# RMSNorm with repeated rows: squares in wide instructions, whole-tile copies on ScalarE, gamma on the loads' queue

## The chip, the cores and the metric

The kernel runs on one core of one Trainium2 chip. The time is that of one execution on the device, in microseconds (us). The kernel before takes 239.57 us (median of 3 runs, 239.40 to 239.84). A profile covers one execution; its span is some 2 us shorter than the time of the same run (237.9 and 239.72 us for the kernel before). A transfer is issued to a queue, moves as packets, and lands: in these traces a whole load is 128 packets of 32 KiB, a store 128 packets of 64 KiB, and each has 16 landing records. The profile counts 16 DMA engines, and this text reads the 16 records as one for each.

## The reference

```python
def reference(x, gamma):                      # x: 8 x 512 x 2048, gamma: 2048, fp32
    x_rep = np.repeat(x, 2, axis=1)           # each row twice
    rms = np.sqrt((x_rep ** 2).mean(axis=-1, keepdims=True) + 1e-6)
    return (x_rep / rms * gamma[None, None, :]).astype(np.float32)
```

It reads 33.6 MB and writes 67.1 MB. There are 4096 rows to normalise; each is written twice.

## The kernel before

Eight tiles of 128 partitions and 4 rows each. A tile's buffer has 8 rows per partition: `x` is loaded into the upper 4, the results go to rows 0, 2, 4, 6 and are then copied to rows 1, 3, 5, 7. There are three buffers, so load 3 waits for store 0 (load 3 is issued at 52.84 us, store 0's last landing record is at 52.82), load 4 for store 1, and so on.

```python
    def square(i, k):                # ScalarE: sum of squares of one row, then the root
        sq = junk.tile([P, D], f32, name="sq")            # in PSUM
        nc.scalar.activation(out=sq[:], in_=ys[i][:, K * (R - 1) + k, :],
                             func=Act.Square, accum_out=ss[:])
        nc.scalar.activation(out=rms[:], in_=ss[:], func=Act.Sqrt, scale=inv_d, bias=eps_t[:])
        # ... cut: allocation of ss, rms and rstd; square returns rms
    def scale(i, k, rms):            # VectorE: x * (1/rms) * gamma
        nc.vector.reciprocal(out=rstd[:], in_=rms[:])
        nc.vector.scalar_tensor_tensor(out=ys[i][:, R * k, :], in0=ys[i][:, K * (R - 1) + k, :],
                                       scalar=rstd[:], in1=gamma_b[:], op0=Alu.mult, op1=Alu.mult)
    def compute(i):
        for k in range(K):
            scale(i, k, square(i, k))
        repeat(i, 0, K // 2, nc.scalar.copy)
        repeat(i, K // 2, K, nc.vector.tensor_copy)
    # ... cut
    load(0, nc.sync, parts=2)
    for c0, c1 in zip(cuts, cuts[1:]):                    # 7 pieces of gamma, ScalarE's queue
        nc.scalar.dma_start(out=gamma_b[0:1, c0:c1], in_=gamma[c0:c1].partition_broadcast(1))
    nc.gpsimd.partition_broadcast(out_ap=gamma_b[:], in_ap=gamma_b[0:1, :])
    # ... cut: eps_t
    load(1, nc.sync); load(2, nc.sync)                    # (two lines in the source)
    loads_after = {2: (3, 4, 5), 4: (6, 7)}
    for i in range(ntiles):
        compute(i)
        store(i, 0, K)
        for j in loads_after.get(i, ()):
            load(j, nc.sync)
```

So the one queue of the sync engine carries, in this order: loads 0, 1, 2, stores 0, 1, 2, loads 3, 4, 5, stores 3, 4, loads 6, 7, stores 5, 6, 7.

## Time and profile before

| | before |
|---|---|
| time, median | 239.57 us |
| span of the profiled run | 237.9 us |
| VectorE (DVE) busy | 96.5 us, 41% |
| ScalarE (ACT) busy | 101.0 us, 42% |
| loads' and stores' queue, share of 16 DMA engines | 98.5% |
| rate over the span | 423 GB/s |

The prediction below shows the page, the stretches and the chain. The timeline of the sync engine's queue: start, length, line, what was issued and how many times.

```profile
27.05 24.67 SPq L56 DMA_DIRECT2D out_dram<-y  x3
52.84 39.05 SPq L52 DMA_DIRECT2D y<-in_x_dram  x3
115.86 12.72 SPq L56 DMA_DIRECT2D out_dram<-y  x2
140.24 19.73 SPq L52 DMA_DIRECT2D y<-in_x_dram  x2
```

Store 3 is issued at 115.86 and store 4 some 12.4 us later; their first packets move at 119.4 and 138.7 us, so both are there in time. The table by stretches (columns: length, busy time of VectorE, ScalarE and GpSimd with the number of instructions, clock, DMA share, GB/s) at 176 to 178 us, where load 7 ends and store 5 begins:

```profile
176.00:178.00 2.00, 1.96 (x3) 2.00 (x3) 0.00 (x0) 1.00 1.43 606
```

A packet is booked whole in the stretch in which it begins. The 606 GB/s are therefore no rate; they say that many of the 64 KiB packets of store 5 (10 by the packet records) began within these 2 us, beside the last 17 of load 7.

### The profile page before, as it was taken

How to read it: one execution, taken by the hardware profiler on the slowest of the kernel's cores; microseconds unless marked ns; L12 is line 12 of the kernel's file. 1: busy time of each engine (PE TensorE's matmuls, PEld its weight loads, DVE VectorE, ACT ScalarE, POOL GpSimd, SP SyncE). 2: the span in 40 equal slices, each digit the busy share in tenths (PEclk: the TensorE clock that was granted, in tenths of full speed). 3: DMA queues.
4: the chain of work that ended last, by engine and by line, in shares of the span. 5: the costliest groups of instructions: out<-in, count | busy, mean ns of one | idle time of the engine just before them, and what ended most of it. 6: DMA issues, size and time to landing. Idle time of an engine off the chain costs nothing.

```text
span 237.9 us, 287 instructions
## 1 busy us (share of the span) xinstructions
DVE 96.5 (41%) x73; ACT 101.0 (42%) x106; POOL 2.5 (1%) x5
## 2 busy tenths in 40 slices
DVE  0049999960000000059999960000199990000000
ACT  2697999900000000099999920000599960000000
POOL 0030000000000000000000000000000000000000
DMA  7999998989899998999998999989998989999994
GB/s 265 436 446 441 441 441 353 530 353 496 386 452 430 397 485 353 441 441 441 441 518 364 464 419 430 452 369 430 435 518 364 518 364 485 397 452 430 408 474 176
DMA packets 2464, 100.69 MB, mean 423 GB/s; under 512 B 279, under 2 KB 285, under 8 KB 286
## 3 DMA queue, kind: packets, MB, share of 16 engines
q1 hardware_dynamic: 2448, 100.66, 98.5%
q14 instruction: 2, 0.02, 0.0%
q10 hardware_dynamic: 14, 0.01, 0.0%
HBM read 33.56 MB, written 67.11 MB: 423 GB/s over the span
## 4 chain that ended last, share of the span: by engine, by line
DMA 58%; ACT 12%; DVE 9%; issue 1%; POOLq 1%; ACTq 1%; SPq 0%
DMA y<-in_x_dram 33%; DMA out_dram<-y 21%; ACT sq L64 8%; DVE y L74 7%; DMA gamma_b<-in_gamma_dram 4%; ACT y L81 3%; DVE y L81 2%; ACT rms L68 1%; POOLq L136 1%; ACTq L95 1%; DVE rstd L73 0%; POOLq L96 0%; SPq L56 0%
## 5 line engine op out<-in xcount | busy, mean ns | idle before, releaser
L64 ACT ACTIVATE sq<-y 128x2048 f32<-128x2048 f32 x32 | 59.7, 1865 | 87.8 <-DMA y<-in_x_dram 87.8
L74 DVE SCALAR_TENSOR_TENSOR y<-y,rstd,gamma_b 128x2048 f32<-128x2048 f32 x32 | 75.3, 2352 | 4.1 <-POOL gamma_b L96 3.0
L73 DVE RECIPROCAL rstd<-rms 128x1 f32<-128x1 f32 x32 | 5.0, 158 | 94.6 <-ACT rms L68 94.3
L81 ACT COPY y<-y 128x4096 f32<-128x4096 f32 x8 | 28.7, 3590 | 1.4 <-DVE y L74 1.4
L81 DVE COPY y<-y 128x4096 f32<-128x4096 f32 x8 | 18.3, 2294 | 0.3
L68 ACT ACTIVATE rms<-ss,eps_t 128x1 f32<-128x1 f32 x32 | 9.4, 295 | 1.0
L64 ACT ACTIVATION_READ_ACCUMULATOR sq<-y 128x1 f32 x32 | 6.0, 187 | 0.0
L64 ACT ACT_TABLE_LOAD x1 | 1.3, 1283 | 3.0 <-issue 3.0
L96 POOL PARTITION_BROADCAST gamma_b<-gamma_b x1 | 2.3, 2294 | 12.2 <-DMA y<-in_x_dram 12.2
L68 ACT ACT_TABLE_LOAD x1 | 1.3, 1283 | 0.0
L98 DVE MEMSET eps_t<- 128x1 f32 x1 | 0.1, 59 | 0.8 <-PEq L125 0.8
L125 POOL MEMSET const-uint8-127<- 128x1 uint8 x1 | 0.1, 102 | 0.0
L125 POOL MEMSET const-bfloat16-1.0<- 128x1 bf16 x1 | 0.1, 101 | 0.0
L125 POOL MEMSET const-float32-0.0<- 128x1 f32 x1 | 0.1, 98 | 0.2 <-issue 0.2
L125 POOL MEMSET const-float32-1.0<- 128x1 f32 x1 | 0.1, 98 | 0.0
## 6 DMA issues: line engine op xcount, KB each, us to landing
y<-in_x_dram SPq DMA_DIRECT2D x7, 4096.0 KB, 14.6
y<-in_x_dram SPq DMA_DIRECT2D x2, 2048.0 KB, 7.4
out_dram<-y SPq DMA_DIRECT2D x8, 24.4
gamma_b<-in_gamma_dram ACTq DMA_DIRECT2D x6, 1.0 KB
gamma_b<-in_gamma_dram ACTq DMA_DIRECT2D x1, 2.0 KB
```

The source lines that it names most:

```text
L64: nc.scalar.activation(out=sq[:], in_=ys[i][:, K * (R - 1) + k, :], func=Act.Square, accum_out=ss[:])
L68: nc.scalar.activation(out=rms[:], in_=ss[:], func=Act.Sqrt, scale=inv_d, bias=eps_t[:])
L73: nc.vector.reciprocal(out=rstd[:], in_=rms[:])
L74: nc.vector.scalar_tensor_tensor(out=ys[i][:, R * k, :], in0=ys[i][:, K * (R - 1) + k, :], scalar=rstd[:], in1=gamma_b[:], op0=Alu.mult, o ...
L81: copy(out=y_r[:, k0:k1, 1, :], in_=y_r[:, k0:k1, 0, :])
L95: nc.scalar.dma_start(out=gamma_b[0:1, c0:c1], in_=gamma[c0:c1].partition_broadcast(1))
L96: nc.gpsimd.partition_broadcast(out_ap=gamma_b[:], in_ap=gamma_b[0:1, :])
L98: nc.vector.memset(eps_t, eps)
L125: nc = _bacc.Bacc("TRN2", target_bir_lowering=False, num_devices=1)
L136: with _tile.TileContext(nc) as tc:
```

## The change

Its intent is fewer and longer instructions. Tiles 2, 5, 7 ("wide") are squared by one instruction of 8192 elements into the free lower half of their own buffer, and VectorE sums them. Tiles 1, 4, 6 ("half") do this for two rows and keep the accumulating square (one instruction that squares a row and sums it) for the other two. Tiles 0 and 3 ("rows") keep four accumulating squares, with one root for two rows. ScalarE takes over nearly all copies. Gamma's pieces go on the loads' queue: six between the halves of tile 0's load, the seventh behind them.

```diff
-    def square(i, k):
+    def total(i, k, ss):                       # accumulating square of one row, to PSUM
+    def square(i, k0, k1):                     # rows k0..k1 in one instruction, to SBUF
+        nc.scalar.activation(out=ys[i][:, k0:k1, :],
+                             in_=ys[i][:, x_at + k0 : x_at + k1, :], func=Act.Square)
+    def reduce(i, k0, k1, ss):
+        nc.vector.tensor_reduce(out=ss[:, k0:k1], in_=ys[i][:, k0:k1, :], op=Alu.add, ...)
+    def rows_tile(i, copy=nc.vector.tensor_copy):
+        for k0 in (0, H):
+            for k in range(k0, k0 + H):
+                total(i, k, ss)
+            rsqrt(k0, k0 + H, ss, rstd)
+            scale(i, k0, k0 + H, rstd)
+        repeat(i, 0, H)
+        repeat(i, H, K, copy)
 ... (cut: half_tile, wide_tile, rsqrt)
-    load(0, nc.sync, parts=2)
+    load_half(y0, 0)
+    for c0, c1 in zip(cuts[:-2], cuts[1:-1]):
+        gamma_piece(c0, c1)                    # on nc.sync
+    load_half(y0, 1)
+    gamma_piece(cuts[-2], cuts[-1])
-    for i in range(ntiles):
-        compute(i)
-        store(i, 0, K)
+    rows_tile(0);  store(0, 0, K)
+    half_tile(1);  square(2, 0, K);  repeat(1, 0, K);  store(1, 0, K)
+    wide_tile(2);  repeat(2, 0, K);  store(2, 0, K)
+    load(3), load(4), load(5)
+    rows_tile(3);  store(3, 0, K)
+    half_tile(4);  square(5, 0, K);  repeat(4, 0, H);  repeat(4, H, K);  store(4, 0, K)
+    load(6), load(7)
+    wide_tile(5);  repeat(5, 0, K);  store(5, 0, K)
 ... (cut: tiles 6 and 7 likewise; several statements are put on one line here)
```

More of the change, by code (lines that the diff above doesn't have):

```diff
@@ L43, with load_half, load @@
     ys = []
-    def load(i, eng, parts=1):
+    def load_half(y, h):
+        k0 = h * (K // 2)
+        at = K * (R - 1) + k0
+        nc.sync.dma_start(out=y[:, at : at + K // 2, :], in_=x_t[0, :, k0 : k0 + K // 2, :])
+    def load(i):
         y = rows.tile([P, K * R, D], f32, name="y")
-        step = K // parts
-        for k in range(0, K, step):
-            at = K * (R - 1) + k
-            eng.dma_start(out=y[:, at : at + step, :], in_=x_t[i, :, k : k + step, :])
+        nc.sync.dma_start(out=y[:, K * (R - 1) :, :], in_=x_t[i])
         ys.append(y)
@@ L59, in store @@
         )
-    def square(i, k):
+    def total(i, k, ss):
         sq = junk.tile([P, D], f32, name="sq")
-        ss = small.tile([P, 1], f32, name="ss")
         nc.scalar.activation(
-            out=sq[:], in_=ys[i][:, K * (R - 1) + k, :], func=Act.Square, accum_out=ss[:]
+            out=sq[:], in_=ys[i][:, K * (R - 1) + k, :], func=Act.Square, accum_out=ss[:, k : k + 1]
         )
-        rms = small.tile([P, 1], f32, name="rms")
-        nc.scalar.activation(out=rms[:], in_=ss[:], func=Act.Sqrt, scale=inv_d, bias=eps_t[:])
-        return rms
@@ L71, in scale @@
-    def scale(i, k, rms):
-        rstd = small.tile([P, 1], f32, name="rstd")
-        nc.vector.reciprocal(out=rstd[:], in_=rms[:])
-        nc.vector.scalar_tensor_tensor(
-            out=ys[i][:, R * k, :], in0=ys[i][:, K * (R - 1) + k, :], scalar=rstd[:], in1=gamma_b[:],
-            op0=Alu.mult, op1=Alu.mult,
-        )
-    def repeat(i, k0, k1, copy):
+    def square(i, k0, k1):
+        x_at = K * (R - 1)
+        nc.scalar.activation(
+            out=ys[i][:, k0:k1, :], in_=ys[i][:, x_at + k0 : x_at + k1, :], func=Act.Square
+        )
@@ new lines, in reduce, with rsqrt, scale @@
+    def reduce(i, k0, k1, ss):
+        nc.vector.tensor_reduce(
+            out=ss[:, k0:k1], in_=ys[i][:, k0:k1, :], op=Alu.add, axis=mybir.AxisListType.X
+        )
+    def rsqrt(k0, k1, ss, rstd):
+        nc.scalar.activation(
+            out=rstd[:, k0:k1], in_=ss[:, k0:k1], func=Act.Sqrt, scale=inv_d, bias=eps_t[:]
+        )
+        nc.vector.reciprocal(out=rstd[:, k0:k1], in_=rstd[:, k0:k1])
+    def scale(i, k0, k1, rstd):
+        for k in range(k0, k1):
+            nc.vector.scalar_tensor_tensor(
+                out=ys[i][:, R * k, :], in0=ys[i][:, K * (R - 1) + k, :], scalar=rstd[:, k : k + 1],
+                in1=gamma_b[:], op0=Alu.mult, op1=Alu.mult,
+            )
@@ L80, in repeat, with columns @@
+    def repeat(i, k0, k1, copy=nc.scalar.copy):
         y_r = ys[i].rearrange("p (k r) d -> p k r d", r=R)
         copy(out=y_r[:, k0:k1, 1, :], in_=y_r[:, k0:k1, 0, :])
-    def compute(i):
-        for k in range(K):
-            scale(i, k, square(i, k))
-        repeat(i, 0, K // 2, nc.scalar.copy)
-        repeat(i, K // 2, K, nc.vector.tensor_copy)
+    H = K // 2
+    def columns():
+        return small.tile([P, K], f32, name="ss"), small.tile([P, K], f32, name="rstd")
+    def rows_tile(i, copy=nc.vector.tensor_copy):
+        ss, rstd = columns()
+        for k0 in (0, H):
[5 more added lines that the diff above has]
+        repeat(i, H, K, copy)
@@ L90, with half_tile, wide_tile @@
+    def half_tile(i):
+        ss, rstd = columns()
+        square(i, H, K)
+        for k in range(H):
+            total(i, k, ss)
+        reduce(i, H, K, ss)
+        rsqrt(0, K, ss, rstd)
+        scale(i, 0, K, rstd)
+    def wide_tile(i):
+        ss, rstd = columns()
+        reduce(i, 0, K, ss)
+        rsqrt(0, K, ss, rstd)
+        scale(i, 0, K, rstd)
     ctx.enter_context(tc.manual_schedule())
-    load(0, nc.sync, parts=2)
     gamma_b = singles.tile([P, D], f32, name="gamma_b")
@@ L93, with gamma_piece @@
     cuts = [0, *range(D // 4, D + 1, D // 8)]
-    for c0, c1 in zip(cuts, cuts[1:]):
-        nc.scalar.dma_start(out=gamma_b[0:1, c0:c1], in_=gamma[c0:c1].partition_broadcast(1))
+    def gamma_piece(c0, c1):
+        nc.sync.dma_start(out=gamma_b[0:1, c0:c1], in_=gamma[c0:c1].partition_broadcast(1))
+    y0 = rows.tile([P, K * R, D], f32, name="y")
+    ys.append(y0)
+    load_half(y0, 0)
[3 more added lines that the diff above has]
+    gamma_piece(cuts[-2], cuts[-1])
@@ L98 @@
     nc.vector.memset(eps_t, eps)
-    load(1, nc.sync)
-    load(2, nc.sync)
+    load(1)
+    load(2)
     assert ntiles == 8
-    loads_after = {2: (3, 4, 5), 4: (6, 7)}
-    for i in range(ntiles):
-        compute(i)
-        store(i, 0, K)
-        for j in loads_after.get(i, ()):
-            load(j, nc.sync)
+    rows_tile(0)
+    store(0, 0, K)
+    half_tile(1)
+    square(2, 0, K)
+    repeat(1, 0, K)
+    store(1, 0, K)
+    wide_tile(2)
+    repeat(2, 0, K)
+    store(2, 0, K)
+    for j in (3, 4, 5):
+        load(j)
+    rows_tile(3)
+    store(3, 0, K)
+    half_tile(4)
+    square(5, 0, K)
+    repeat(4, 0, H)
+    repeat(4, H, K)
+    store(4, 0, K)
+    for j in (6, 7):
+        load(j)
+    wide_tile(5)
+    repeat(5, 0, K)
+    store(5, 0, K)
+    half_tile(6)
+    square(7, 0, K)
+    repeat(6, 0, H)
+    repeat(6, H, K)
+    store(6, 0, K)
+    wide_tile(7)
+    repeat(7, 0, H)
+    repeat(7, H, K)
+    store(7, 0, K)
 _INS = ['x', 'gamma']
```

## The prediction

The forecast's sums came to about 116 us for ScalarE and about 121 us for VectorE, and its time to 239.6 us. VectorE's term for the six new reductions is cut, since no trace before the change shows such an instruction; the 121 us and the issue times of stores 1, 2, 4, 6 and 7 still contain it. The 7.0 us for a ScalarE instruction of 8192 elements stay as an estimate, because the groups of the page give it too: 1865 ns for 2048 elements and 3590 ns for 4096 are 0.842 ns for each further element, hence 7.04 us for 8192. The times from issue to first byte and from last byte to landing are those of the trace: the first packet moves at 1.61 us, 0.9 us after the first issue; the 16 last packets end at 235.37 to 236.76 us, the 16 landing records of store 7 are at 235.76 to 237.11.

> **What bounds the kernel now.** I read the page first (engine shares, DMA queues), then the issue times of the DMA queue in the timeline, then the chain of waits, and last the busy table by stretches. The page:
>
> ```profile
> span 237.9 us, 287 instructions
> DVE 96.5 (41%) x73; ACT 101.0 (42%) x106; POOL 2.5 (1%) x5
> q1 hardware_dynamic: 2448, 100.66, 98.5%
> HBM read 33.56 MB, written 67.11 MB: 423 GB/s over the span
> ```
>
> Both compute engines are idle more than half of the time, while the queue that carries loads and stores keeps its 16 engines busy for 98.5% of the span. The table by stretches (columns: length, busy time of DVE, ACT and POOL, clock, DMA share, GB/s) shows where that is not so:
>
> ```profile
> 1.00:1.50 0.50, 0.00 (x0) 0.00 (x0) 0.00 (x0) 1.00 0.00 0
> ...
> 52.80:101.10 48.30, 0.00 (x0) 0.00 (x0) 0.00 (x0) 1.00 0.98 423
> 101.10:140.20 39.10, 35.88 (x27) 36.87 (x39) 0.00 (x0) 1.00 1.02 443
> ...
> 235.40:237.90 2.50, 0.00 (x0) 0.00 (x0) 0.00 (x0) 1.00 0.00 0
> ```
>
> The transfers stop only in the first 1.5 us and the last 2.5 us. In the 48 us of the second line no engine computes at all and the DMA still runs full. The chain of waits gives the rate of the stream (start, duration, what):
>
> ```profile
> 27.05 25.77 DMA out_dram<-y
> ...
> 52.84 48.32 DMA y<-in_x_dram
> ...
> 115.86 24.36 DMA out_dram<-y
> 140.22 0.02 issue
> 140.24 29.08 DMA y<-in_x_dram
> ```
>
> Store 0 lands at 52.82, store 3 at 115.86 + 24.36 = 140.22. Between them go stores 1, 2, 3 (8.389 MB each) and loads 3, 4, 5 (4.194 MB each): 37.75 MB in 87.40 us = 431.9 GB/s, so 19.42 us for a store and 9.71 us for a load. All 100.66 MB at that rate take 233.1 us. The span is 237.9, so only 4.8 us, 2.0%, is not pure stream, and of those about 4 are the head and tail above[...]. **So a gain over 2% is all but impossible; the only question is whether the change opens a hole in the stream.**
>
> [...]423 GB/s with idle engines, 443 with both at over 90%. So more work on ACT and DVE should not slow the transfers.
> [...]
>
> **The change part by part.** Tiles 0 and 3 keep squares by row, 1, 4, 6 become half and half, 2, 5, 7 wide. The durations, from the groups of the page:
>
> ```profile
> L64 ACT ACTIVATE sq<-y 128x2048 f32<-128x2048 f32 x32 | 59.7, 1865 | 87.8 <-DMA y<-in_x_dram 87.8
> L74 DVE SCALAR_TENSOR_TENSOR y<-y,rstd,gamma_b 128x2048 f32<-128x2048 f32 x32 | 75.3, 2352 | 4.1 <-POOL gamma_b L96 3.0
> L81 ACT COPY y<-y 128x4096 f32<-128x4096 f32 x8 | 28.7, 3590 | 1.4 <-DVE y L74 1.4
> L81 DVE COPY y<-y 128x4096 f32<-128x4096 f32 x8 | 18.3, 2294 | 0.3
> L68 ACT ACTIVATE rms<-ss,eps_t 128x1 f32<-128x1 f32 x32 | 9.4, 295 | 1.0
> ```
>
> - Squares: 32 by row become 14 (2x4 + 3x2), 2.05 us each with the accumulator read of 187 ns, = 28.7; 3 of 4096 at 3.6 = 10.8; 3 of 8192 at 7.0 = 21.0. Before 59.7 + 6.0 = 65.7, after 60.5.
> - Square roots: 32 become 10 (4 + 6), 9.4 to 3.0 us on ACT; reciprocals likewise, 5.0 to 1.6 on DVE.
> - Copies: before, 8 halves on ACT (28.7) and 8 on DVE (18.3). After, DVE keeps 2 (4.6) and ACT does the other 14 halves, three of them as whole tiles: 8 x 3.59 + 3 x 7.0 = 49.7.
> - Reductions, new on DVE[...].
> - Sums: ACT 60.5 + 3.0 + 49.7 + 2.6 of table loads = about 116 (from 101); DVE [...]about 121 (from 96.5). Both remain near half of the span: **more work, none of it on the path, if each store is still issued before the stream runs dry**.
>
> That is the test. A store must be issued about 1.4 us before the transfer in front of it lands: its first bytes move about 1.0 us after issue (first issue 0.72, first transfers between 1.5 and 2.0), and landing is told about 0.4 us after the last byte (last byte at 235.4; the last store's landing record 235.8 to 237.1). I laid out the new order engine by engine with the landings before: first half 8.1, second half 13.0, loads 1 to 5 at 22.7, 33.4, 101.2, 110.9, 120.6.
>
> - **Gamma.** The queue's waits before:
>
> ```profile
> SPq L52 <- DMA y<-in_x_dram: 5.7, 1, 5.7
> ...
> SPq L52 <- DMA gamma_b<-in_gamma_dram: 0.9, 1, 0.9
> ```
>
> Load 1 waited 5.7 us for the first half because the completion semaphores are reused after eight transfers (in the trace load 1 carries the first half's semaphore). In the new order the ninth transfer is the last gamma piece, so I expect it to be held until 8.1 and to land behind the second half, near 13.1 (12.4 before). Broadcast and first multiply then come 2.5 us later, at about 15.6 (14.92 before). The six pieces between the halves cost about 6 x 0.27 = 1.6 us of issue, so the second half is issued near 2.8, while the first still flows until about 7.5: no hole.
> - **Tile 0**: multiplies from 15.6, 4 x 2.37 plus one reciprocal, DVE copy 2.3: store 0 at 27.6 (27.05 before). Its limit is load 2's landing 33.4 - 1.4 = 32.0: 4 us to spare.
> - **Tile 1** (half): [...]root and reciprocal to 32.7, four multiplies to 42.1, whole copy on ACT 7.0: store 1 at 49.2 (39.2 before). Limit: store 0's landing, 52.8 (its earliest engine 0.7 less), minus 1.4 = 50.7 to 51.4: **1.5 us to spare**.
> - **Tile 2** (wide): [...]multiplies from 51.4 to 60.8, copy to 67.9: store 2 there. Limit one store later, about 70.3: 2.4 us.
> - **Tile 3** (rows): lands 101.2; two squares and one root to 105.6, multiplies to 110.5 and, after the second root, to 115.4, DVE copy: store 3 at 117.7 (115.86 before). Limit: load 5's landing 120.6 (earliest engine 119.9) - 1.4 = 118.5: **0.8 us to spare**, the tightest.
> - **Tile 4** (half): reduce from 117.7, multiplies to 132.1, ACT squares tile 5 (122.5 to 129.5) and then copies two halves to 136.7: store 4 there. Limit 140.2 (earliest 139.2) - 1.4 = 137.8: 1.1 us.
> - **Tiles 5, 6, 7**: store 5 ready at about 158, but it queues behind load 7, which waits for store 4's landing near 159.6; store 6 near 193.4 and store 7 near 209.6, against limits of 197 and 216. Room everywhere.
>
> No store misses its limit, so the sum of the effects on the end is zero.
>
> **The rivals.**
> - *A new wait takes over.* With margins of 0.8 to 1.5 us at stores 1, 3 and 4, a duration wrong by some 5% over a tile opens a hole[...]. For it: no reduce or wide square has been measured here.[...] It would cost 0.3 to 1.5 us: 240 to 241.[...]
> - *ACT or DVE becomes the bound.* 116 and 121 us of work against 233 us of stream: no, except through the local order above.
> - *Gamma's move helps or hurts.* Seven issues leave ACT[...]; the first store has 4 us of room, so neither an earlier nor a later gamma shows. 239.3 to 239.8.
>
> **Range and chances.** The three runs before span 239.4 to 239.84. I expect **239.6 us**, range **239.1 to 240.7**, longer on the slow side for the tight stores. Faster by over 2% would need 234.8, and the stream alone plus head and tail needs about 237: 0.01. Slower by over 2% needs a hole of 4.8 us: 0.03. The same: 0.96.
>
> **What would show it.** Right: the DMA share stays near 98.5%; the mean rate near 423 GB/s; stores 1 and 2 issued near 49 and 68 instead of 39 and 51[...]; the last gamma piece issued near 8.1. Wrong: a stretch without transfers near 51, 71, 119 or 138 us;[...] a last gamma piece or first store so late that the stream stops near 32 us.

## More of the kernel before

The stream of data changes from reading to writing three times (load 2 to store 0, load 5 to store 3, load 7 to store 5) and from writing to reading twice (store 2 to load 3, store 4 to load 6).

## The result, and the profile after

The changed kernel takes 240.49 us (6 runs, 240.18 to 240.73) against 239.59 us (239.40 to 239.91) of the kernel before: ratio 1.0036, 95% interval 1.0024 to 1.0049. A ratio here is the mean time of one kernel's fast runs over that of the other's of the same rounds, so not quite the ratio of the medians. By the 2% measure it is the same; but it is clearly a little slower, by 0.9 us.

The page of the changed kernel, the same lines as before:

```profile
span 239.0 us, 219 instructions
DVE 119.3 (50%) x51; ACT 114.1 (48%) x57; POOL 2.5 (1%) x5
q1 hardware_dynamic: 2462, 100.67, 98.5%
HBM read 33.56 MB, written 67.11 MB: 421 GB/s over the span
```

Both compute engines work more, and the queue is as busy as ever: 98.5%. That share says only that packets are under way: it is 98.5% in both kernels, although some packets of this one took up to 2.3 us in place of 1.2, as shown below. The groups, with different shapes kept apart:

```profile
L77 DVE TENSOR_REDUCE ss<-y 128x4 f32<-128x8192 f32 x3 | 26.0, 8681 | 0.0
L72 ACT ACTIVATE y<-y 128x8192 f32<-128x8192 f32 x3 | 21.1, 7024 | 3.8 <-DMA y<-in_x_dram 3.8
L96 ACT COPY y<-y 128x8192 f32<-128x8192 f32 x3 | 21.1, 7017 | 20.3 <-DVE y L89 20.3
L77 DVE TENSOR_REDUCE ss<-y 128x2 f32<-128x4096 f32 x3 | 13.3, 4419 | 22.6 <-ACT y L72 22.6
```

The sums took 8681 and 4419 ns, the wide square 7024 ns and the whole copy 7017 ns, against the 7.0 us of the prediction for these two; the square of 4096 took 3613 ns, against 3.6 us. The queue's timeline:

```profile
8.04 0.22 SPq L136 DMA_DIRECT2D gamma_b<-in_gamma_dram  x1
8.30 0.82 SPq L54 DMA_DIRECT2D y<-in_x_dram  x2
27.40 40.17 SPq L58 DMA_DIRECT2D out_dram<-y  x3
67.66 24.46 SPq L54 DMA_DIRECT2D y<-in_x_dram  x3
117.67 19.05 SPq L58 DMA_DIRECT2D out_dram<-y  x2
139.97 19.95 SPq L54 DMA_DIRECT2D y<-in_x_dram  x2
160.02 49.74 SPq L58 DMA_DIRECT2D out_dram<-y  x3
```

Store 0 went out at 27.40, store 3 at 117.67, store 4 at 136.38 (the trace's issue record within the fifth line). The stream never ran dry: from 2.5 to 235 us at least 13 packets were under way at any moment (at least 14 before). But the span grew by 1.0 us (237.94 to 238.95; an expectation below has 1.1, from the rounded spans). Where is that microsecond? The landing records of the trace (first and last of the 16 DMA engines) locate it:

| landing | before, us | after, us |
|---|---|---|
| load 5 | 119.88 to 120.58 | 119.98 to 120.63 |
| store 3 | 139.19 to 140.22 | 139.28 to 139.95 |
| store 4 | 158.78 to 159.61 | 159.04 to 159.56 |
| load 6 | 168.17 to 169.32 | 168.40 to 169.22 |
| **load 7** | **177.88 to 179.12** | **178.59 to 180.09** |
| store 7 | 235.76 to 237.11 | 236.60 to 238.12 |

Up to load 6 the two agree to about 0.3 us. Load 7 takes 9.71 us before and 10.19 us after from first landing to first landing (9.72 and 10.31 us in the mean of the 16 engines), and its last engine lands 1.0 us later; that microsecond is still there at the end (238.12 against 237.11). The stretch shown above for the kernel before, in the changed one:

```profile
176.00:178.00 2.00, 1.55 (x2) 1.14 (x3) 0.00 (x0) 1.00 1.06 311
```

311 in place of 606: with the engines under way the whole time (share 1.06), fewer packets began, because those of load 7 took longer. The packet records give it directly. The median 32 KiB load packet took 1.213 us in both profiles. At this change from reading to writing, 16 of the last ones took 1.6 to 2.3 us (the records do not tell on which engine). Summed over all load packets that began at 174 to 178 us and divided by 16, the excess is 0.71 us an engine, against 0.05 us before. I call this sum **the excess at 176**. The last packets of store 4, at 154 to 158 us, show a smaller one, 0.17 us against 0.02. The remaining 0.2 us are at the change from load 2 to store 0, which is slow in both kernels (1.16 us an engine against 0.94) and varies between 0.87 and 1.16 us over all the profiles below.

### The profile page after: what moved, and what is told of

Its sections match the earlier page's. It is cut to its first block, busy times and chain, and to the rows that moved or that the text cites. A ratio compares the mean times of both kernels' runs of the same rounds, so it can differ in the third digit from the quotient of the medians.

```text
span 239.0 us, 219 instructions
## 1 busy us (share of the span) xinstructions
DVE 119.3 (50%) x51; ACT 114.1 (48%) x57; POOL 2.5 (1%) x5
## 3 DMA queue, kind: packets, MB, share of 16 engines
q1 hardware_dynamic: 2462, 100.67, 98.5%
## 4 chain that ended last, share of the span: by engine, by line
DMA 38%; DVE 36%; ACT 8%; issue 3%; POOLq 1%; SPq 1%; ACTq 0%
DMA y<-in_x_dram 26%; DVE y L89 22%; DVE ss L77 11%; DMA out_dram<-y 9%; ACT y L96 4%; DMA gamma_b<-in_gamma_dram 3%; DVE y L96 2%; ACT sq L65 2%; ACT y L72 2%; POOLq L212 1%; ACT rstd L82 1%; SPq L136 1%; DVE rstd L85 0%; SPq L50 0%; SPq L58 0%
## 5 line engine op out<-in xcount | busy, mean ns | idle before, releaser
L89 DVE SCALAR_TENSOR_TENSOR y<-y,rstd,gamma_b 128x2048 f32<-128x2048 f32 x32 | 74.0, 2349 | 2.3 <-POOL gamma_b L146 1.7
L96 ACT COPY y<-y 128x4096 f32<-128x4096 f32 (+1 forms) x11 | 49.7, 4531 | 29.1 <-DVE y L89 29.1
L77 DVE TENSOR_REDUCE ss<-y 128x2 f32<-128x4096 f32 (+1 forms) x6 | 39.3, 6550 | 22.6 <-ACT y L72 22.6
L65 ACT ACTIVATE sq<-y 128x2048 f32<-128x2048 f32 x14 | 26.2, 1874 | 40.3 <-DMA y<-in_x_dram 40.1
L72 ACT ACTIVATE y<-y 128x4096 f32<-128x4096 f32 (+1 forms) x6 | 31.9, 5319 | 15.6 <-DMA y<-in_x_dram 15.6
L85 DVE RECIPROCAL rstd<-rstd 128x4 f32<-128x4 f32 (+1 forms) x10 | 1.7, 171 | 60.7 <-ACT rstd L82 60.7
L82 ACT ACTIVATE rstd<-ss,eps_t 128x4 f32<-128x4 f32 (+1 forms) x10 | 3.0, 297 | 9.5 <-DVE ss L77 9.4
L96 DVE COPY y<-y 128x4096 f32<-128x4096 f32 x2 | 4.6, 2294 | 0.1
L65 ACT ACTIVATION_READ_ACCUMULATOR sq<-y 128x1 f32 x14 | 2.6, 186 | 0.0
```

Of the source, the lines that this page charges most:

```text
L72: nc.scalar.activation(out=ys[i][:, k0:k1, :], in_=ys[i][:, x_at + k0 : x_at + k1, :], func=Act.Square)
L77: nc.vector.tensor_reduce(out=ss[:, k0:k1], in_=ys[i][:, k0:k1, :], op=Alu.add, axis=mybir.AxisListType.X)
L82: nc.scalar.activation(out=rstd[:, k0:k1], in_=ss[:, k0:k1], func=Act.Sqrt, scale=inv_d, bias=eps_t[:])
L85: nc.vector.reciprocal(out=rstd[:, k0:k1], in_=rstd[:, k0:k1])
L96: copy(out=y_r[:, k0:k1, 1, :], in_=y_r[:, k0:k1, 0, :])
```

## The experiments

Twelve kernels, all with the correct result, each timed in 5 rounds against the kernel before on the same chip.

### Does it come back, and which half of the change brings it?

One profile can show an accident, so both kernels went again. Beside them the change was split: gamma's move alone, and the compute alone.

```diff
 gamma only (on the kernel before)
-    load(0, nc.sync, parts=2)
-    ... 7 gamma pieces on nc.scalar
+    load_half(y0, 0); 6 gamma pieces on nc.sync; load_half(y0, 1); 1 gamma piece on nc.sync

 compute only (on the changed kernel)
+    load_half(y0, 0); load_half(y0, 1)
+    ... 7 gamma pieces on nc.scalar, as in the kernel before
```

The kernel before, again:

> The kernel before, unchanged, against itself: ratio 1.000 within 0.15% and about 239.6 us. Its second profile tells whether the packets at the change from load 2 to store 0 (32 KiB load packets of 1.5 to 2.3 us in place of 1.21, about 0.9 us an engine) and the quick change from load 7 to store 5 (under 0.1 us) come back: if both do, they belong to the kernel; if they move, a single profile cannot carry the explanation.

The changed kernel, again:

> The changed kernel, unchanged: ratio about 1.0036, about 240.5 us. In its first profile load 7's last packets took up to 2.3 us in place of 1.21 (0.7 us an engine) where store 5 follows, and that was nearly all of the 1.1 us by which the span grew. Theory A (this slow change from reading to writing belongs to the changed kernel): it is there again. Theory B (it falls in any run by chance): it is gone or sits elsewhere, and the span is still longer for another reason.

Gamma only:

> Kernel before with only gamma's pieces moved onto the loads' queue, the compute unchanged. If the loss comes from the queue's head (theory G), ratio 1.0036, 240.5 us. If it comes from the new compute order (theory C), 1.000, 239.6 us, and store 0 issued near 27.5.

Compute only:

> Changed kernel with gamma's pieces back on ScalarE's queue behind both halves, all the new compute kept. Theory C: 1.0036, 240.5 us. Theory G: 1.000, 239.6 us. If each part costs half, both this and the gamma-only run stand near 1.0018.

Measured: before again 1.0001 (0.9989 to 1.0013); after again 1.0055 (1.0042 to 1.0069); gamma only 1.0015 (1.0003 to 1.0027); compute only 1.0038 (1.0025 to 1.0051). The stretch at 176 to 178 us in the changed kernel's second profile, then in the compute-only one, then in the gamma-only one:

```profile
176.00:178.00 2.00, 1.54 (x3) 0.76 (x3) 0.00 (x0) 1.00 1.13 360
```

```profile
176.00:178.00 2.00, 1.54 (x3) 0.89 (x3) 0.00 (x0) 1.00 1.18 393
```

```profile
176.00:178.00 2.00, 1.96 (x3) 2.00 (x3) 0.00 (x0) 1.00 1.57 672
```

The slow packets come back (excess 0.59 and 0.55 us) wherever the new compute is, and are absent (0.04 us) where the old is. So they belong to the kernel, and theory B, the accident, falls. Most of the loss is the new compute's. Gamma's move costs at most some 0.3%; its interval barely clears zero. In its profile the last DMA engine lands 0.96 us behind the last but one, and three single packets were delayed by 0.33 to 0.46 us (the records do not tell on which engine); in the two profiles of the kernel before the last engine trails by 0.2 and 0.5 us, and one of these packets, at 134.5 us, is late there too (0.35 and 0.43 us). Whether gamma's move causes that was not tested.

### Which tiles?

The new compute was put back tile by tile, with gamma as before: new for tiles 0 to 2, for 3 to 5, or for 6 and 7, old elsewhere.

```diff
 new in 3, 4, 5:
-    rows_tile(0) ... wide_tile(2) ... half_tile(6) ... wide_tile(7)
+    old form for tiles 0, 1, 2, 6, 7; rows_tile(3), half_tile(4), wide_tile(5) as changed
```

> Gamma as before, the new compute for tiles 0, 1, 2 only, the old one for 3 to 7. In three profiles with all the new compute the last load packets before store 5 took about 0.6 us an engine longer (none in three profiles with the old compute), and the last packets of store 4 about 0.05 to 0.17 us. Theory C1 (compute that runs while the queue changes from one direction to the other holds the packets up): tiles 0 to 2 are done by then, so ratio 1.000 and no slow change at 176 us. Theory C2 (the loss is carried in from the head, such as later stores 1 and 2): 1.003 or more.

> Gamma as before, the new compute for tiles 3, 4, 5 only. Here ScalarE's whole copy of tile 5 lies beside the change from store 4 to load 6 (154 to 159 us). If the loss starts there: slow store packets at 154 to 157 us, then also a slow change at 176 us[...], ratio about 1.003. If the loss belongs to the compute that runs at 176 us (tile 6): ratio 1.000 to 1.001 and a quick change at 176 us.

> Gamma as before, the new compute for tiles 6 and 7 only. If tile 6's squares to SBUF, reduction and the wait between them make the change at 176 us slow: load 7's last packets about 0.6 us an engine over 1.21 us, ratio about 1.003. If not: quick change, ratio 1.000.

Measured: tiles 0 to 2, 0.9998 (0.9986 to 1.0010); tiles 3 to 5, 1.0036 (1.0020 to 1.0051); tiles 6 and 7, 0.9998 (0.9985 to 1.0011). All of the compute's loss is in tiles 3 to 5. The stretch for tiles 3 to 5, then for tiles 6 and 7:

```profile
176.00:178.00 2.00, 1.97 (x3) 1.97 (x3) 0.00 (x0) 1.00 0.92 279
```

```profile
176.00:178.00 2.00, 1.55 (x2) 1.14 (x3) 0.00 (x0) 1.00 1.64 705
```

These two lines are worth a second look. In the first, VectorE and ScalarE do exactly the old work of tile 6, and the packets are slow. In the second they do the new work, with the same busy times as in the changed kernel (1.55 and 1.14), and the packets are fast. So it is not the compute that runs beside the slow packets. Theory C1 falls, and C2 with it, since the new tiles 0 to 2 cost nothing: something is carried over from tiles 3 to 5.

### Three ideas for what is carried over

In tiles 3 to 5 I saw three differences that could reach the DMA: ScalarE copies tile 5 until 158 us, beside the change from store 4 to load 6 (theory D); store 4 is issued 8 us later (theory E); or something else. Copies of the same values to the same place make it possible to try the first two without any other change.

```diff
 extra copies of tile 5 (old compute otherwise; ScalarE works from 141 to 158 us)
+    repeat(5, 0, K); repeat(5, 0, K); repeat(5, 0, H)       # before store(5, 0, K)

 late store 4 (old compute otherwise)
+    repeat(4, 0, K)                                         # before store(4, 0, K)

 quick tile 5 (on the run with tiles 3, 4, 5 new)
-    repeat(5, 0, K)
+    repeat(5, 0, H); repeat(5, H, K, nc.vector.tensor_copy)
```

> Gamma and compute as before, but ScalarE copies tile 5's rows twice and a half more (the same values to the same place), from about 141 to 158 us, before store 5 is issued; store 5 waits behind load 7 until 160 anyway. Theory D (an engine that copies in SBUF beside the change from store 4 to load 6 slows packets, and the loss follows): slow store packets at 154 to 157, slow load packets at 176, ratio about 1.003. Theory E (what matters is that store 4 is issued 8 us later): as the kernel before, 1.000.

> Gamma and compute as before, but ScalarE copies tile 4 once more, so that store 4 is issued near 135 in place of 128 us and tile 5 is done near 150: no engine works at 151 to 158. Theory D: 1.000 and quick changes at 154 and 176. Theory E: ratio about 1.003 with the slow load packets at 176.

> The run with the new compute in tiles 3, 4, 5 (1.0036), but tile 5's copy halved: ScalarE the first half as soon as its rows are there, VectorE the second, done near 153 in place of 158 us. Theory D: the changes at 154 and 176 are quick again, ratio 1.000 to 1.001. Theory E: 1.003 as before, since store 4 is as late.

Measured: extra copies 1.0004 (0.9992 to 1.0016), with ScalarE copying for 17.70 us from 140.72 and an excess at 176 of 0.09 us; late store 4, 1.0002 (0.9989 to 1.0015), with store 4 issued at 135.23 as intended and an excess of 0.03 us; quick tile 5, 1.0043 (1.0026 to 1.0061), excess 0.58 us. In the last, nothing computes between 152.6 and 169 us, and still the last packets of store 4 are slow from 155.7 us on, and load 7's later. Its stretch:

```profile
176.00:178.00 2.00, 1.97 (x3) 1.97 (x4) 0.00 (x0) 1.00 0.95 295
```

**Both D and E fall** as causes by themselves. Neither copies beside the change of direction nor a late store 4 brings the loss, and taking the copies away does not remove it. Whether a late store 4 is needed beside something else was not tested. What is left of the difference is tile 3, and what tiles 4 and 5 do before 152 us.

### Tile 3

Tile 3's new form ends later than the old one: store 3 goes out at 117.67 in place of 115.86 us, some 2 us in place of 3.6 us before the first packet of store 3 moves (119.4 to 119.5 in the packet records).

```diff
 late store 3 (old compute otherwise)
+    repeat(3, 0, 1)                                         # before store(3, 0, K)

 old tile 3 (on the compute-only run, all other tiles new)
-    rows_tile(3)
+    tile 3 in the old form: one root a row
```

> Gamma and compute as before, but ScalarE copies one row of tile 3 once more (same values), so that store 3 is issued near 117.8 in place of 115.9 us, as in the changed kernel. Theory F (store 3's later issue, so shortly before the loads in front of it end, sets off the slow packets at 154 and 176): ratio about 1.003. Theory G2 (the new compute of tiles 4 and 5 does, through something other than the times of issue): 1.000 and quick changes.

> All the new compute with gamma as before (1.0038), but tile 3 in the old form, with its store issued near 115.8 us. Theory F: ratio 1.000 to 1.001 and no slow packets at 154 and 176. Theory G2: 1.003 to 1.004 with the slow packets as in the run it is taken from.

Late store 3 **did not do what it was built for**. ScalarE made the extra copy while VectorE was still copying the second half, so store 3 was issued at 115.87 us, not 117.8; only store 4 moved, to 130.19. Its 1.0009 (0.9996 to 1.0023) and excess of 0.11 us say nothing about theory F.

Old tile 3 gave a clear answer: 0.9996 (0.9984 to 1.0009), with five runs within 239.41 to 239.53 us. The change of this one tile takes the whole of the 0.38% away. The two runs were on different chips, but on this run's chip quick tile 5 had shown the loss (1.0043). Its queue and its stretch:

```profile
115.81 20.45 SPq L58 DMA_DIRECT2D out_dram<-y  x2
139.92 19.91 SPq L54 DMA_DIRECT2D y<-in_x_dram  x2
```

```profile
176.00:178.00 2.00, 1.54 (x3) 0.99 (x3) 0.00 (x0) 1.00 1.46 623
```

Store 3 is issued early again (115.81), store 4 is as late as in the changed kernel (135.91), and the packets at 176 us are fast: excess 0.05 us. So theory G2 falls: the new tiles 4 and 5 are not enough. The run came out as theory F forecast, but that does not show F, since the other instructions of tile 3 went back together with the time of its store.

### All fourteen profiles together

| kernel | store 3 issued, us | excess at 154 (stores) | excess at 176 (loads) | ratio |
|---|---|---|---|---|
| before, first and again | 115.86, 115.86 | 0.02, 0.00 | 0.05, 0.01 | 1, 1.0001 |
| gamma only | 115.74 | 0.00 | 0.04 | 1.0015 |
| new in 0, 1, 2 | 115.69 | 0.00 | 0.09 | 0.9998 |
| new in 6, 7 | 115.85 | 0.00 | 0.02 | 0.9998 |
| extra copies of tile 5 | 115.91 | 0.00 | 0.09 | 1.0004 |
| late store 4 | 115.77 | 0.00 | 0.03 | 1.0002 |
| late store 3 (as it came out) | 115.87 | 0.00 | 0.11 | 1.0009 |
| old tile 3, rest new | 115.81 | 0.02 | 0.05 | 0.9996 |
| after, first and again | 117.67, 117.52 | 0.17, 0.11 | 0.71, 0.59 | 1.0036, 1.0055 |
| compute only | 117.31 | 0.05 | 0.55 | 1.0038 |
| new in 3, 4, 5 | 117.85 | 0.13 | 0.67 | 1.0036 |
| quick tile 5 | 117.51 | 0.14 | 0.58 | 1.0043 |

Excesses are in us an engine. No profile is an exception, and the landing records say the same without any packet: load 7 lands 9.72 to 9.80 us after load 6 (mean of the 16 engines) in the first nine, 10.17 to 10.31 us in the other five. What is shown: most of the loss lies in load 7's slow packets at the change to store 5; it came in the five profiles, of four kernels, in which tiles 3, 4 and 5 all have their new form, with store 3 at 117.3 to 117.9 us, and in no other; it goes when tile 3 alone goes back. **What stays open:** whether the later issue of store 3 or the other instructions of tile 3 set it off, since no run moved one without the other; whether tile 3 alone would suffice without the new tiles 4 and 5 and their later store 4; and how something at 118 us slows packets 36 to 60 us later, while at 118 us itself hardly any is (at most 0.04 us an engine in all of them).

## Why the prediction was right or wrong

**The forecast of no change over 2%, and the range, were right.** 240.49 lies within 239.1 to 240.7, and the case against a gain over 2% held: the stream is the bound and was already full (98.5%). That the time fell inside the range is partly luck: the point forecast was 239.6, and the slow side had been made wide for holes in the stream, of which none came.

**The layout of the new order was right, step by step.** Predicted and measured issue of the stores: store 0 at 27.6 and 27.40, store 1 at 49.2 and 48.74, store 2 at 67.9 and 67.24, store 3 at 117.7 and 117.67, store 4 at 136.7 and 136.38, store 6 at 193.4 and 194.23, store 7 at 209.6 and 209.43. The sums came out at 114.1 us for ScalarE (about 116 predicted) and 119.3 for VectorE (about 121). The last gamma piece was held as expected: it waited 4.6 us for the first half of tile 0's load, whose semaphore (one of eight) it carries in the trace, and was issued at 8.04 (8.1) and landed at 13.13 (13.1). No store missed its limit.

**The step that failed** is the one from there to the time: "No store misses its limit, so the sum of the effects on the end is zero." The sum was 0.9 us, not zero, though no limit was missed. The step took for granted that a stream that is never dry always moves at the same rate: 19.42 us a store, 9.71 us a load. It nearly does in steady flow (19.3 and 9.7 us from landing to landing), but not at every change of direction. Load 7 took 10.19 us (first landing to first landing), and the last DMA engine lost 1.0 us. The trace that the prediction had before it already held such a place: load 2, in front of store 0, landed 10.5 us after load 1, not 9.71, in a stream that was never dry; those 0.8 us are about what the prediction's sum (4.8 less about 4 for head and tail) left over. The layout of issues has no term for this; why the new tile 3 sets it off at load 7 stays open.

**The rivals.** The first, "a new wait takes over", named the right size (0.3 to 1.5 us) for the wrong reason: it needed a hole, and there was none. That ACT or VectorE would become the bound did not happen: they were busy for 114.1 and 119.3 us of 239.0. Gamma's move was put at 239.3 to 239.8 us; alone it measured 239.78, at the upper end, against 239.38.

**The signs.** Of the signs that stand there for a right prediction, every one was seen, and of those for a wrong one none. The DMA share was named as a sign and is useless here: it is 98.5% in both kernels, because the share counts the time that packets took, and load 7's slow packets (1.6 to 2.3 us) count in full. The landing-to-landing time of each transfer would have been the sign to name.

## What to carry to other kernels

When the transfers are the bound, check first that each store is issued before the stream reaches it; that could be laid out here to within 0.9 us (0.03 to 0.83 us off) from the durations and rates of a profile, except for the sums, whose durations no trace had shown yet. A full DMA queue was not yet a fast one here (98.5% in both kernels, with load 7 at 9.71 and 10.19 us): compare the time of each transfer, landing to landing, between the two kernels, and look at the changes between loads and stores. And when a loss shows up at one place, put back one group of tiles at a time before believing in the work that happens to run beside it: here the slow packets fell beside tile 6, and putting back tile 3 was enough to remove them.
